# Three orders around the second layer of a two-layer trunk: the last chunk's 1/rms, the spatial mix's banks and the out-projection's parts

## The chip, the core and the metric

The kernel runs on one core of a Trainium2 chip. The metric is the time of one execution in microseconds of device time; the kernel before has a median of 1097.71 us over three runs (1096.62 to 1098.31).

## The reference

1024 prompt tokens and 64 sample tokens, 1088 columns in all, go through two layers and a final RMSNorm. Layer 0 is sparse attention beside a short convolution; layer 1 is a chunked gMLP with a spatial gating unit. What the change touches is the end of layer 0 and all of layer 1:

```python
x = x + gate[:, None] * out                       # end of layer 0
h = _rmsnorm(x, norm_g[1]) * (1 + scale[:, None]) + shift[:, None]
u, v, g = _split(h @ w_in, (SGU_DIM, SGU_DIM, SGU_DIM))
u = jax.nn.gelu(u)
v = _layernorm(jax.nn.gelu(v), ln_g, ln_b)
wm = jnp.tril(ws[:, :lc, :lc])                    # one 128x128 matrix for each of 8 groups
s = jnp.einsum('gij,bnjgc->bnigc', wm, vc) + bs[:, :lc].T[None, None, :, :, None]
out = (u * s * jax.nn.silu(g)) @ w_out
x = x + gate[:, None] * out                       # then the final RMSNorm
```

## The kernel before, in words

Features lie on the 128 partitions, tokens along the free dimension; a tensor of 1024 features is eight slices of 128. Every fp32 operand of a large product is kept as two parts, a high part in fp32r (ScalarE copies it, line 295) and a low part, the difference (VectorE, line 296); a product is three passes, high by high, high by low and low by high. `ah` and `al` hold the two parts of the current activations, 8 slices by 1088 columns.

The program is written in the order of the algorithm, and a planner decides the order of each engine's queue by a simulated time: an earlier instruction of the program goes first if the planner thinks that it is ready, else a later one. `manual_schedule` takes one engine out of this: its instructions stand in the order written. `issue_after(x)` keeps what is written under it behind instruction x. Each engine then runs its queue strictly in order.

**End of layer 0.** `out_projection(0, ...)` (line 1133 on) works on columns 0 to 448, 448 to 832 and 832 to 1088 (chunks 0, 1, 2). For each chunk and each of 8 output tiles come 24 products, the residual on VectorE (line 1153), a square on ScalarE (lines 1156, 1159) and a running sum of the squares on GpSimd (line 1161). `rstd` then sums over the partitions with products against a column of ones (line 229), scales on VectorE (232), takes the power -0.5 on GpSimd (233) and spreads the result over the partitions with transposes (235). `h1` normalises the chunk (lines 1176 to 1181: VectorE, GpSimd, ScalarE, VectorE for each slice) into `ah`, `al` and, in fp32, into the residual's own tiles.

**Sums.** Products of layer 1 after the first two output tiles are made with Strassen's scheme (Winograd's form) on 2 by 2 blocks: seven products in place of eight, of half the depth. The input side needs four sums of blocks: `sums` (VectorE, lines 1220 to 1223) forms them in place, and `sum_parts` splits them into the tiles T1, T2, T3 and, for the fourth, into `ah` and `al`. They come in four pieces of columns, of which the one that reaches into the last chunk is the largest (1024 elements a partition); the other three need only chunks 0 and 1.

**Entry of layer 1.** The first two output tiles (`two`) are made plainly with `project`, 24 products for each of the column ranges 0 to 364, 364 to 728 and 728 to 1088; only the last range needs chunk 2. Then the memory of the residuals is released (`self.resid.close()`), and tiles of layer 1 lie in it, among them S0, S1 and S2, in which `pair_weights` (line 1263, `p_s`) builds the weight sums of the Strassen products. `pair` makes two output tiles with seven products of two halves each ("st", line 1291). Its products go through the PSUM banks "pj", "lg" and "pt" in turn, two banks each.

**Spatial mix.** `v` is transposed to rows, normalised block by block (`layernorm`: statistics on VectorE, power on GpSimd, one product of a column on VectorE, line 1348, and the scaling on ScalarE, line 1351), and `spatial` multiplies, for each of 8 groups, nine blocks by the group's matrix into two banks tagged "lg" and a small one. VectorE evicts them with scale and bias (line 1372); for groups 0 to 3 it goes to an S tile, the same of the three for all parts of a group, and VectorE multiplies it into the gate (line 1374).

**Out-projection of layer 1.** The last pairs make the u tiles, and VectorE multiplies each quarter into the gate product `gs` (line 1466). Then all eight slices of chunk 0, of chunk 1 and of chunk 2 are split into `ah` and `al`, in this order of the program, and `out_projection(1, ...)` runs. Its weights' low parts are made on GpSimd (line 256). The first product of a pair reads slices 0 to 3 of column quarters 0 and 2 of `ah` and `al`, the second slices 4 to 7 of the same quarters, the sixth and the seventh the same slices of quarters 1 and 3; a quarter is 272 columns. The residuals of chunks 1 and 2 are loaded again over SP's queue into tiles that free up at the end.

Of the kernel before, what the change touches and what calls it, by code (L numbers as in the profile page):

```python
# [17 lines left out]
P = 128  # L18
D = 1024
KT = D // P  # L20
# [19 lines left out]
def pieces(w):  # L40

    return [*range(0, w - P, P), w - P]
# [52 lines left out]

OUT_KTS = (4, 5, 6, 7, 0, 1, 2, 3)


# [9 lines left out]
class Trunk:  # L108
# [112 lines left out]

    def rstd(self, name, w, *accs):

        nc = self.nc
        pt = self.bank("pt", name)
        n = len(pieces(w))
        for j, o in enumerate(pieces(w)):
            for i, acc in enumerate(accs):
                nc.tensor.matmul(pt[:, w + j:w + j + 1], acc[:, o:o + P], self.ones, start=i == 0,
                                 stop=i == len(accs) - 1)  # L230
        r = self.small.tile([P, 4], F32, tag="rs", name="rs", bufs=3)
        nc.vector.tensor_scalar(r[:, 0:n], pt[:, w:w + n], 1.0 / D, EPS, op0=OP.mult, op1=OP.add)
        nc.gpsimd.tensor_tensor(r[:, 0:n], r[:, 0:n], self.nhalf[:, 0:n], op=OP.pow)
        for j, o in enumerate(pieces(w)):
            nc.tensor.transpose(pt[:, o:o + P], r[:, j:j + 1].to_broadcast([P, P]), self.ident)
        return pt[:, 0:w]

# [898 lines left out]
    def out_projection(self, l, ws, after):  # L1136
# [4 lines left out]
        for c in range(NCH):  # L1141
# [4 lines left out]
            for t in range(KT):  # L1146
# [10 lines left out]
                else:  # L1157
                    sq = self.column("sq")[:, 0:w]
                    nc.scalar.activation(sq, x[:, t, :], AF.Square)
                    if t < KT - 1 or c < NCH - 1:  # L1160
# [4 lines left out]
            if l == 0:  # L1165
                self.load(self.spill[c], x)
        after(NCH - 1, self.rstd("rstd", *accs[-1]))

# [184 lines left out]
    def spatial(self, g, gs, times):  # L1353

        nc = self.nc
        vt, c = self.vtok[g // 4], slice(g % 4 * P, (g % 4 + 1) * P)
        pt = [self.ps.tile([P, 512], F32, tag="lg", name="sgu_ps", bufs=2) for _ in range(2)]
        for n in range(NBLK):
# [4 lines left out]
        parts = [(slice(a * 512, a * 512 + 512), pt[a].rearrange("p (b c) -> p b c", c=P),  # L1363
                  self.bs[:, g, None, :].to_broadcast([P, 4, P])) for a in range(2)]
        for s, p, b in (*parts, (slice(SO, SO + DEC), ps[:, 0:DEC], self.bs[:, g, 0:DEC])):
            y = gs[:, s]
            if times:
                u = self.l1.tile([P, 512], F32, tag=f"S{g % 3}", name="sgu")[:, 0:s.stop - s.start]
            else:
                u = y  # L1370
            o = u.rearrange("p (b c) -> p b c", c=P) if s.stop <= SEQ else u
            nc.vector.scalar_tensor_tensor(o, p, self.lngb[:, 0, g:g + 1], b, op0=OP.mult, op1=OP.add)
            if times:
                nc.vector.tensor_mul(y, y, u)

    def layer1(self, es):
# [17 lines left out]
        two = [self.weights(w1[t]) for t in range(2)]  # L1394
        for cs in (range(NCH - 1), (NCH - 1,)):
            for t in range(2):
                self.project(two[t], gelu(t), cs)
        self.sum_parts((2, 1, 3))
        self.sum_parts((4,))
        self.resid.close()  # L1400
# [63 lines left out]
        for n, t in enumerate((*range(KT + 4, 2 * KT, 2), *range(2 * KT, 3 * KT, 2))):  # L1464
            def times(src, k, s):
# [4 lines left out]
                                                             name="w_1") if t < 6 else None) for t in range(KT)]  # L1470
        for c in range(NCH):
            s = slice(*OUT_CHUNKS[c])
            for t in range(KT):
                self.split(self.ah[:, t, s], self.al[:, t, s], gs[t][:, s])
        for c in range(1, NCH):
            xc.append(r2.tile([P, KT, w[c]], F32, tag=f"v{c % 2}", name=f"x{c}"))
            self.load(xc[c], self.spill[c])
# [12 lines left out]
    def run(self):  # L1490
        with ExitStack() as es:
# [9 lines left out]
            with self.pool("held", "right") as self.held:  # L1501
# [18 lines left out]
                with self.pool("wo", "right") as wp:  # L1520
# [10 lines left out]
                    with self.tc.issue_after(self.lastav):  # L1531
                        self.out_projection(0, ws, self.h1)
                    self.sums()
            self.layer1(es)
# [72 lines left out]
```

## Time and profile before

| | |
|---|---|
| Median of three runs | 1097.71 us |
| Profiled execution | 1095.83 us, span 1094.1 us |
| Busy: TensorE / VectorE / ScalarE / GpSimd | 1050.8 / 738.5 / 592.5 / 493.5 us |
| Granted TensorE clock | 0.993 of full speed |
| Entry of layer 1 | about 691 to 728 us |
| Spatial mix | about 836 to 860 us |
| End of the last pair, start of the out-projection | about 979 to 1000 us |

In the rows below PE is TensorE, DVE VectorE, ACT ScalarE, POOL GpSimd and SP the engine that issues the transfers. An L number is the line of the kernel that issued the instruction; lines 264 and 295/296 belong to helpers that several stages use, so there the tile's name tells which stage it is. `idle before` is time in which the engine did nothing just before the instruction, and the name behind the arrow is what ended it.

### The profile page before, as it was taken

What the parts mean: (1) busy time and instruction counts of PE and PEld (TensorE: products, weight loads), DVE (VectorE), ACT (ScalarE), POOL (GpSimd) and SP (SyncE); (2) the same over time, 40 slices, a digit from 0 to 9 for tenths busy, and PEclk for the clock granted to TensorE, in tenths of its full rate; (3) what the DMA queues carried; (4) which work ended last, traced back from release to release, by engine and by line L of the source; (5) the groups of instructions that cost most, each with busy time, mean ns of one, the idle gap of its engine ahead of it and who ended that gap; (6) DMA issues with size and microseconds to landing.
All of it is one profiled execution on the core that took longest, in us unless ns stands there. A gap on an engine that the chain in (4) does not pass through costs nothing.

```text
span 1094.1 us, 20011 instructions
## 1 busy us (share of the span) xinstructions
PE 1050.8 (96%) x7523; PEld 1013.6 (93%) x7523; DVE 738.5 (67%) x1849; ACT 592.5 (54%) x1152; POOL 493.5 (45%) x519
## 2 busy tenths in 40 slices
PE   4899999999999989999999999989999999999996
PEld 4889778999999989999999999989999999998996
DVE  5610789998887786777787445685568876667134
ACT  5643488775776597767787323543346244354111
POOL 1014224345864655535458246464334344454322
PEclk9899999999999999999999999999999999999998
DMA  9754711121110111000001622031111311124012
GB/s 366 300 202 155 261 31 36 66 77 39 40 39 21 39 58 30 12 21 20 20 20 40 243 85 97 39 97 59 40 39 31 121 44 43 66 87 154 1 68 96
DMA packets 31776, 90.30 MB, mean 83 GB/s; under 512 B 5568, under 2 KB 11968, under 8 KB 28480
## 3 DMA queue, kind: packets, MB, share of 16 engines
q1 hardware_dynamic: 31680, 89.03, 23.0%
q8 instruction: 59, 0.97, 0.4%
q14 instruction: 37, 0.30, 0.1%
HBM read 78.44 MB, written 10.58 MB: 81 GB/s over the span
## 4 chain that ended last, share of the span: by engine, by line
PE 83%; DVE 9%; ACT 3%; issue 2%; DMA 1%; POOL 1%; SPq 0%; POOLq 0%; DVEq 0%; ACTq 0%
PE st L1291 20%; PE pj L264 20%; PE op L264 15%; PE pj L281 9%; PE av L731 3%; PE logit_ps L687 3%; PE p_ps L713 3%; PE ada_ps L168 2%; PE first L336 2%; PE score_ps L451 1%; DVE al L296 1%; DVE cum L647 1%; PE score_ps L452 1%; DMA x<-in_x 1%; DVE bias L648 1%
## 5 line engine op out<-in xcount | busy, mean ns | idle before, releaser
L256 POOL TENSOR_TENSOR w_lo<-w_raw,w_hi 128x1024 fp32r<-128x1024 f32 x35 | 84.2, 2407 | 160.0 <-ACT w_hi L255 158.0
L264 PE MATMUL pj<-ah,w_hi 128*128 128x364 f32 (+1 forms) x456 | 150.3, 331 | 1.0 <-ACT w_hi L255 1.0
L264 PE MATMUL pj<-al,w_hi 128*128 128x364 f32 (+1 forms) x456 | 150.3, 330 | 0.7 <-DVE al L1181 0.7
L264 PE MATMUL pj<-ah,w_lo 128*128 128x364 f32 (+1 forms) x456 | 149.2, 329 | 0.0
L1291 PE MATMUL st<-ah,p_w 128*128 128x272 f32 x704 | 137.3, 290 | 0.6 <-ACT ring L1390 0.6
L553 DVE TENSOR_SCALAR_CACHE_REDUCE junk<-S,cand 128x512 bf16<-128x512 f32 (+5 forms) x142 | 119.0, 838 | 1.9
L1291 PEld LDWEIGHTS st<-ah,p_w 128*128 128x128 f32 x704 | 111.7, 188 | 1.7 <-ACT ring L1390 0.9
L1258 POOL TENSOR_TENSOR p_w<-p_s,p_w 128x512 fp32r<-128x512 f32 x44 | 58.9, 1341 | 85.7 <-ACT p_w L1257 85.6
L281 PE MATMUL pj<-ah,w_lo 128*128 128x364 f32 (+1 forms) x288 | 95.7, 332 | 0.0
L281 PE MATMUL pj<-ah,w_hi 128*128 128x364 f32 (+1 forms) x288 | 95.5, 332 | 0.0
L281 PE MATMUL pj<-al,w_hi 128*128 128x364 f32 (+1 forms) x288 | 95.3, 331 | 0.0
L580 ACT ACTIVATE junk<-S,cand 128x896 bf16<-128x896 f32 (+2 forms) x78 | 77.7, 996 | 29.5 <-DVE m L583 25.8
L1291 PE MATMUL st<-al,p_w 128*128 128x272 f32 x352 | 92.8, 291 | 0.0
L1153 DVE SCALAR_TENSOR_TENSOR x<-op,mod,x 128x192 f32<-128x192 f32 (+2 forms) x64 | 30.2, 496 | 91.5 <-PE op L264 87.4
L264 PEld LDWEIGHTS pj<-ah,w_hi 128*128 128x128 f32 x456 | 85.6, 188 | 2.0 <-ACT w_hi L255 1.3
L264 PEld LDWEIGHTS pj<-al,w_hi 128*128 128x128 f32 x456 | 85.7, 188 | 1.3 <-DVE al L1181 1.3
L264 PEld LDWEIGHTS pj<-ah,w_lo 128*128 128x128 f32 x456 | 85.6, 188 | 0.2 <-issue 0.2
L264 PE MATMUL op<-ah,w 128*128 128x448 f32 (+2 forms) x336 | 82.4, 330 | 0.8 <-ACT ah L295 0.8
L694 POOL TENSOR_SCALAR S<-S,sm 128x128 f32<-128x128 f32 (+8 forms) x68 | 51.3, 759 | 67.8 <-DVE sm L693 55.9
L1258 POOL TENSOR_TENSOR p_w<-p_raw,p_w 128x512 fp32r<-128x512 f32 x33 | 47.0, 1425 | 47.5 <-ACT p_w L1257 47.5
L1291 PEld LDWEIGHTS st<-al,p_w 128*128 128x128 f32 x352 | 66.3, 188 | 0.3 <-issue 0.2
L264 PE MATMUL op<-ah,w_hi 128*128 128x384 f32 (+2 forms) x200 | 65.1, 326 | 0.0
(320 smaller groups left out, 2998.2 us busy)
## 6 DMA issues: line engine op xcount, KB each, us to landing
ada<-in_ada_w SPq DMA_DIRECT2D x19, 1024.0 KB, 7.8
w_raw<-in_w SPq DMA_DIRECT2D x31, 512.0 KB, 3.5
p_raw<-in_w SPq DMA_DIRECT2D x44, 256.0 KB, 3.0
w_raw<-in_wo SPq DMA_DIRECT2D x16, 512.0 KB, 3.5
x<-in_x SPq DMA_DIRECT2D x8, 544.0 KB, 6.3
bo<-in_ada_w SPq DMA_DIRECT2D x4, 1024.0 KB, 6.7
x<-in_x SPq DMA_DIRECT2D x1, 1792.0 KB, 7.8
spill<-x SPq DMA_DIRECT2D x1, 1792.0 KB, 5.7
```

What stands on the lines that cost most here:

```text
L256: (nc.gpsimd if lo_eng == "pool" else nc.vector).tensor_sub(lo, raw, hi)
L264: last = self.nc.tensor.matmul(ps, wt[:, kt, :], at[:, kt, c0:c1], start=n == 0, stop=n == len(mms) - 1)
L281: self.nc.tensor.matmul(ps, wt[:, kt, :], at[:, kt, a:b], start=kt == 0 and i == 0, stop=kt == KT - 1 and i == 2)
L553: V.tensor_scalar(junks[0][:, 0:SW[j]], self.S[:, span(j)], thr, 0.0, op0=OP.is_lt, op1=OP.add, accum_out=col(cv, j))
L580: nc.scalar.activation(junks[1][:, 0:SW[j]], self.S[:, span(j)], AF.Sign, scale=-1.0, bias=col(cand, j), accum_out=col(cv, j))
L687: nc.tensor.matmul(pt[:, 0:w], lhs, keys[i][:, t // 2, s], start=i == 0, stop=i == 1)
L694: self.lastnorm = nc.gpsimd.tensor_scalar(p, p, st[:, 3:4], 0.5, op0=OP.mult, op1=OP.mult).ins
L713: nc.tensor.transpose(pt[0:r, o:o + P], p[:, j * P:j * P + r], self.ident)
L731: self.lastav = nc.tensor.matmul(av[:, 0:m], self.vs[0:r, vbase + j, t // 2, :], part[0:r, x:x + m], start=j == 0 and i == 0, stop=(j + 1) ...
L1153: nc.vector.scalar_tensor_tensor(x[:, t, a:b], ps[:, a:b], self.mod[l][:, 16 + t, j:j + 1], x[:, t, a:b], op0=OP.mult, op1=OP.add)
L1258: nc.gpsimd.tensor_sub(w[:, 1], src, w[:, 0])
L1291: nc.tensor.matmul(ps, w[:, p, k, :], at[:, k, :], start=i == 0, stop=i == len(mms) - 1)
```

## The change

It has three parts.

First, the end of `rstd` is split: `rstd_steps` stops between the power and the transposes. For layer 0, `out_projection` no longer normalises the last chunk but hands the unfinished `rstd_steps` to layer 1. There the 24 products of the first output tile and the first column range are written out for TensorE one by one; after the seventh come the sums for 1/rms, after the nineteenth the transposes. `h1` of the last chunk and `sums` follow. The other five groups of 24 products come in the order (tile 0, range 1), (1, 0), (1, 1), (0, 2), (1, 2), and all parts of the sums are held behind the last square (`lastsq`), T2 first, then T3, T1 and the fourth.

Second, in `spatial` the odd groups use the two "pj" banks, the multiply into the gate (groups 0 to 3) runs on GpSimd, and the S tiles go round for each part and not for each group.

Third, the parts of chunk 0 for the out-projection are made in two cuts, columns 0 to 272 and 272 to 448, for slices 0 to 5, and whole for slices 7 and 6; the parts of chunks 1 and 2 are held behind the last high part of chunk 0 (`lasthi`).

```diff
+RSTD = (6, 18)
-    def rstd(self, name, w, *accs):
+    def rstd(self, *args):
+        *_, rb = self.rstd_steps(*args)
+        return rb
+
+    def rstd_steps(self, name, w, *accs):
...
         nc.gpsimd.tensor_tensor(r[:, 0:n], r[:, 0:n], self.nhalf[:, 0:n], op=OP.pow)
+        yield
         for j, o in enumerate(pieces(w)):
             nc.tensor.transpose(pt[:, o:o + P], r[:, j:j + 1].to_broadcast([P, P]), self.ident)
-        return pt[:, 0:w]
+        yield pt[:, 0:w]
...
-                    nc.scalar.activation(sq, x[:, t, :], AF.Square)
+                    self.lastsq = nc.scalar.activation(sq, x[:, t, :], AF.Square).ins
...
+        if l == 0:
+            return self.rstd_steps("rstd", *accs[-1])
         after(NCH - 1, self.rstd("rstd", *accs[-1]))
...
-        pt = [self.ps.tile([P, 512], F32, tag="lg", name="sgu_ps", bufs=2) for _ in range(2)]
+        pt = [self.ps.tile([P, 512], F32, tag="pj" if g % 2 else "lg", name="sgu_ps", bufs=2) for _ in range(2)]
...
+        n = g
         for s, p, b in (*parts, (slice(SO, SO + DEC), ps[:, 0:DEC], self.bs[:, g, 0:DEC])):
             y = gs[:, s]
             if times:
-                u = self.l1.tile([P, 512], F32, tag=f"S{g % 3}", name="sgu")[:, 0:s.stop - s.start]
+                n += 1
+                u = self.l1.tile([P, 512], F32, tag=f"S{n % 3}", name="sgu")[:, 0:s.stop - s.start]
...
             if times:
-                nc.vector.tensor_mul(y, y, u)
+                nc.gpsimd.tensor_mul(y, y, u)
...
         two = [self.weights(w1[t]) for t in range(2)]
-        for cs in (range(NCH - 1), (NCH - 1,)):
-            for t in range(2):
-                self.project(two[t], gelu(t), cs)
-        self.sum_parts((2, 1, 3))
-        self.sum_parts((4,))
+
+        with self.tc.manual_schedule(engines={mybir.EngineType.PE}):
+            for n, _ in enumerate(self.steps(two[0], gelu(0), (0,), n=1)):
+                if n in RSTD:
+                    rb = next(self.late)
+        self.h1(NCH - 1, rb)
+        self.sums()
+        for t, cs in ((0, (1,)), (1, (0, 1)), (0, (2,)), (1, (2,))):
+            self.project(two[t], gelu(t), cs)
+        with self.tc.issue_after(self.lastsq):
+            self.sum_parts((2, 3, 1))
+            self.sum_parts((4,))
...
-        for c in range(NCH):
-            s = slice(*OUT_CHUNKS[c])
-            for t in range(KT):
+
+        a, b = OUT_CHUNKS[0]
+        for s, ts in ((slice(a, Q), range(KT - 2)), (slice(Q, b), range(KT - 2)), (slice(a, b), (KT - 1, KT - 2))):
+            for t in ts:
                 self.split(self.ah[:, t, s], self.al[:, t, s], gs[t][:, s])
+        with self.tc.issue_after(self.lasthi):
+            for c in range(1, NCH):
+                s = slice(*OUT_CHUNKS[c])
+                for t in range(KT):
+                    self.split(self.ah[:, t, s], self.al[:, t, s], gs[t][:, s])
...
                     with self.tc.issue_after(self.lastav):
-                        self.out_projection(0, ws, self.h1)
-                    self.sums()
+                        self.late = self.out_projection(0, ws, self.h1)
```

## Rows read from the trace of the kernel before

**Rows 1.** By stage: length, busy PE, PEld, DVE, ACT, POOL; clock, DMA, GB/s.
```profile
705.00:718.00 13.00, 12.27 (x74) 11.49 (x72) 10.77 (x20) 9.42 (x22) 11.15 (x16) 1.00 0.00 0
718.00:728.00 10.00, 6.81 (x53) 6.44 (x52) 9.93 (x10) 6.84 (x13) 4.98 (x4) 1.00 0.04 11
...
836.00:842.30 6.30, 6.30 (x53) 6.11 (x52) 3.33 (x12) 5.30 (x9) 1.08 (x2) 1.00 0.01 3
842.30:860.00 17.70, 16.16 (x122) 14.44 (x121) 17.67 (x37) 1.89 (x3) 3.84 (x3) 1.00 0.04 12
...
983.00:999.70 16.70, 14.06 (x69) 12.18 (x68) 16.70 (x26) 9.53 (x21) 9.09 (x3) 1.00 0.17 58
999.70:1010.00 10.30, 10.30 (x51) 9.50 (x52) 4.16 (x8) 3.17 (x6) 1.85 (x1) 1.00 0.92 356
```

**Rows 2.** Waits of TensorE: total, times, longest, in 690 to 760 and 836 to 1010.
```profile
PE st L1291 <- ACT p_w L1257: 2.6, 1, 2.6
...
PE op L264 <- DVE al L296: 1.8, 1, 1.8
```

**Rows 3.** Timeline of 691 to 705 (start, duration), TensorE, VectorE, ScalarE, GpSimd.
```profile
691.21 0.33 PE L264 MATMUL pj<-ah,w_hi 128*128 128x364 f32 x1
692.38 0.33 PE L264 MATMUL pj<-al,w_hi 128*128 128x364 f32 x1
...
691.83 0.60 DVE L1153 SCALAR_TENSOR_TENSOR x<-op,mod,x 128x192 f32<-128x192 f32 x2
...
695.16 0.40 ACT L1159 ACTIVATE sq<-x 128x256 f32<-128x256 f32 x1
...
699.67 0.16 DVE L232 TENSOR_SCALAR rs<-rstd 128x2 f32<-128x2 f32 x1 [2.42 <-PE rstd L229]
699.91 0.71 POOL L233 TENSOR_TENSOR rs<-rs,nhalf 128x2 f32<-128x2 f32 x1 [8.69 <-DVE rs L232]
704.16 0.75 DVE L1176 TENSOR_TENSOR t<-x,rstd 128x256 f32<-128x256 f32 x2 [4.33 <-PE rstd L235]
```

**Rows 4.** GpSimd's normalisation by line (busy, mean ns); VectorE's timeline behind it.
```profile
L1179 POOL TENSOR_SCALAR x<-t,modA,mod 128x192 f32<-128x192 f32 (+1 forms) x16 | 11.5, 732 | 4.4 <-DVE t L1176 4.4
...
719.37 2.20 DVE L1223 TENSOR_TENSOR x<-x,x 128x1024 f32<-128x1024 f32 x1
726.36 1.28 DVE L1263 TENSOR_TENSOR p_s<-p_raw 128x512 f32<-128x512 f32 x2
```

**Rows 5.** Timeline around the spatial mix, 820 to 861.
```profile
823.48 1.12 DVE L1348 SCALAR_TENSOR_TENSOR mv<-mv 128x1 f32<-128x1 f32 x1
...
837.46 0.74 DVE L1372 SCALAR_TENSOR_TENSOR sgu<-sgu_ps,lngb,misc 128x512 f32<-128x512 f32 x1
...
838.37 3.10 ACT L1351 ACTIVATE vtok<-vtok,mv 128x512 f32<-128x512 f32 x4
...
857.43 3.01 POOL L1258 TENSOR_TENSOR p_w<-p_s,p_w 128x512 fp32r<-128x512 f32 x2 [2.17 <-ACT p_w L1257]
857.98 0.74 DVE L1372 SCALAR_TENSOR_TENSOR gsb<-sgu_ps,lngb,misc 128x512 f32<-128x512 f32 x1
859.55 1.44 DVE L1263 TENSOR_TENSOR p_s<-p_raw,p_s 128x512 f32<-128x512 f32 x1
```

**Rows 6.** Out-projection: VectorE's timeline, a group by shape, SP's issues, a weight's high part.
```profile
990.26 2.60 DVE L1466 TENSOR_TENSOR gsb<-gsb,u 128x272 f32<-128x272 f32 x1
992.78 5.83 DVE L296 TENSOR_TENSOR al<-gsb,ah 128x448 fp32r<-128x448 f32 x8
...
L296 DVE TENSOR_TENSOR al<-gsb,ah 128x256 fp32r<-128x256 f32 x4 | 3.8, 962 | 0.0
...
1001.15 0.33 SPq L130 DMA_DIRECT2D x<-spill  x1
1001.57 0.39 SPq L130 DMA_DIRECT2D w_raw<-in_wo  x1
...
1010.70 1.06 ACT L255 ACTIVATE w_hi<-w_raw 128x1024 fp32r<-128x1024 f32 x1 [1.75 <-DMA w_raw<-in_wo]
```

## The prediction

> **What bounds the kernel now.** I read the page's busy shares first: TensorE (PE) works nearly all the span, so what this change can win is TensorE's idle time in the stages it touches, and no other engine's busy sum. Next I read busy time by stage [rows 1]: a row whose PE figure equals its length has nothing to give. Idle are 13.00 - 12.27 = 0.73 us in 705 to 718 and 10.00 - 6.81 = 3.19 us in 718 to 728 (entry of layer 1: 3.92 together), 17.70 - 16.16 = 1.54 us in 842.3 to 860 (spatial mix), 16.70 - 14.06 = 2.64 us in 983 to 999.7 (start of the out-projection). The sum is 8.1 us. Last I read who ended the long ones [rows 2]: one wait of 2.6 us for the weights of a Strassen product and one of 1.8 us for a low part of the out-projection. In both VectorE's queue stood ahead, as the timelines show [rows 4, 6].
>
> **Entry of layer 1.** Today the last residual is added at 691.83 (until 692.43), but its square runs on ScalarE at 695.16, behind nine parts of the sums (three small pieces, three parts each); the column sums are out at 699.67, and VectorE starts the last chunk's normalisation at 704.16, though the power on GpSimd takes only 0.71 us from 699.91 [rows 3]. Of the 12.3 us from residual to normalisation little is work. The change keeps the parts off ScalarE until the square has been issued and writes TensorE's order out: seven products, sums, twelve products, transposes, five products. The trace has the first product at 691.21 and the eighth at 692.38 [rows 3], 0.167 us apart; the sums stand in the eighth's place. The square can run at 692.43 and takes 0.40, so the sums can start at about 692.9: TensorE, which can take nothing else now, waits 0.5 us. Bounds: 0 if the residual comes sooner, 3.2 us if the square stays at 695.16 + 0.40. I take 0.5, since the residual's row is the nearest. The sums take some 0.6 us, VectorE's scaling and the power end by 694.7 (from 699.67 to 700.62 they took 0.95 now), and the twelve products cover until 695.5. Normalisation then starts near 695.9 instead of 704.16: 8.2 us sooner.
>
> What is late next: GpSimd's part of the normalisation is 16 instructions at 732 ns, 11.5 us [rows 4]. From 695.9, with the nine small parts now beside it, the last chunk is ready between 708 and 712. TensorE has four groups of 24 products, 4 x 24 x 0.167 = 16 us, before it needs the first slice at about 709 and the eighth at 712.5, so I take 0 for that wait (bounds 0 and 2 us). The 0.73 us go. Then VectorE's train: three large differences and four large parts, seven instructions, one of them 2.20 us at 719.37, ended before p_s at 726.36 [rows 4], because p_s lies where the residual chunks lay. That end was 704.16 + 22.2. From 695.9, plus some 3 us for small parts that used to be done before, it comes at about 721, and ScalarE's copy follows. TensorE reaches the third Strassen product at 691.2 + 144 x 0.167 + 0.5 + 1.0 (sums, transposes) = 716.7 and 48 products of 6.81 / 53 = 0.128 [rows 1] on, about 723. I leave 0.8 us of wait for contention in the train. Stage: 3.92 - 0.5 - 0.8 = 2.6 us gained. Bounds: 3.9, and about 0 (the train ending at 726 as now, 3.4 us of wait beside the 0.5); below nothing I see no way, since the train starts sooner in every case.
>
> **Spatial mix.** Until 842.3 TensorE has no gap [rows 1], because the next pair's first 24 products sit in the two "pj" banks and fill the time until ScalarE has the last normalised block (838.37 + 3.10 = 841.47) [rows 5]. Then seven groups alternate over two "lg" banks, and each waits for VectorE: 1.54 us. Afterwards odd groups take the "pj" banks. So evictions no longer stop TensorE: per group it needs 16.16 / 7 = 2.3 us [rows 1], while VectorE, without the multiply, needs two evictions of 0.74 and a small one, under 1.9. But the filler is gone: the next pair's first product has to wait behind the last odd group. In its place from 838 stand the rest of group 0 and seven eighths of group 1 (about 2.3 us) and, once two evictions are through, the first halves of groups 2 and 3 (2 x 1.0 us): 4.3 us, enough for 841.5. Upper bound of the gain 1.5; lower bound -2.7: without those halves TensorE is dry at 840.3 and stands until 841.5, or until 843.0 if one GpSimd instruction stands before the last scale, and the evictions win nothing. The multiply on GpSimd is not in the trace; the nearest row is its subtraction of the same size, 3.01 / 2 = 1.5 us beside VectorE [rows 5]. Eight and four small ones are 12 to 14 us from 838 to about 852, and three "S" tiles and four banks let VectorE run ahead of them; p_s for the next pair then starts near 852, as today. I take +0.6 us, nearer the upper end, because VectorE's first eviction came at 837.46 [rows 5], well before 841, even today.
>
> Is GpSimd free for this? A p_s of two SBUF tiles took 1.44 us at 859.55 while GpSimd's 3.01 ran, the eviction of a PSUM tile 0.74 at 857.98 beside the same instructions, and a product of one column 1.12 us at 823.48 [rows 5]. The Trainium skill (SBUF — State Buffer, Who interferes with whom) says that a VectorE instruction with two SBUF inputs and a GpSimd instruction that reads SBUF exclude each other for a whole instruction, while one SBUF input does not contend; the trace agrees on both counts, with these numbers. By that rule evictions stay at 0.74 and the layer norm's last one-column product can stand behind a multiply, which is rival D; the sum above would then have -1.2 in place of +0.6.
>
> **Out-projection.** At 983 the last pair's products end. Five banks hold what chunk 0 can do with six of eight slices; then TensorE waits for the low part (1.8) and, for the other 0.8, for the high part of the last slices [rows 1, 2]. VectorE's queue shows why: a gate product at 990.26 took 2.60 us beside GpSimd, and then eight parts, several of them chunk 1's and 2's, took 5.83 us from 992.78, ahead of the last gate products, after which ScalarE could start [rows 6]. The change cuts chunk 0 at column 272: columns 0 to 272 of slices 0 to 5 lie in quarters that only the last pair's first two products read, so these six parts can leave the jam: five products of 24 x 0.128 = 3.1 us lie between them and 983, which puts them at about 968; the rest are narrower. Chunks 1 and 2 (16 parts) may not start before the last high part of chunk 0. The gate products of slices 6 and 7 then go through at about 983 to 985, and TensorE needs their parts only six slices, 18 x 0.202 = 3.6 us (10.30 / 51 each [rows 1]), after 983. All 2.64 us can go; 0 would stay if GpSimd's low weights, which are unchanged, hold VectorE as before. I take 2.4, near the upper end, because what stood ahead is moved behind. Six more instructions on ScalarE and on VectorE lie under products.
>
> Other edits: the S tiles' new rotation and the generator cost nothing by themselves, and the two projections in another order are the same 144 products.
>
> **Sum.** 2.6 + 0.6 + 2.4 = 5.6 us. The profiled execution took 1095.83 us (span 1094.1 and 1.7 around it), 1.9 below the median of three, 1097.71; as a difference the sum stands against either: 1090.2 for an execution like the profiled one, 1092.1 for the median.
>
> **Rivals.**
> A, the forecast: all three stages give most of their idle time, 1092.1, own range 1089 to 1095.
> B, the train stays the bound at the entry: sums and parts slowed by GpSimd end 2 us later, and the wait for the third product's weights keeps 2.6 us. For it: 2.20 us at 719.37 for a difference of 1024 columns beside GpSimd [rows 4]; against: they start 8 us sooner. Gain 3.92 - 0.5 - 2.6 = 0.8, in all 0.8 + 0.6 + 2.4 = 3.8: 1093.9.
> C, the out-projection keeps its 2.64 us: the jam is contention with GpSimd's low weights, for which the 2.60 us at 990.26 speaks; against it, that the parts of chunks 1 and 2 leave the jam. Gain 2.6 + 0.6 = 3.2: 1094.5.
> D, the spatial mix loses: without the filler TensorE is dry from 840.3, and a multiply of 1.5 us ahead of the layer norm's last column puts the last block from 841.5 to 843.0. 2.7 lost, 1.5 won: 2.6 + 2.4 - 1.2 = 3.8: 1093.9. For it speaks that the first eviction ends at 838.2 [rows 5], and its multiply is then ready before that column; against, that two evicted banks give TensorE 2 us more.
> E, slower: the parts of chunks 1 and 2, held back, hold a DMA queue. The load of chunk 2's residual goes into the tile that they read; it was issued at 1001.15, the eighth weight's load right behind it at 1001.57, and that weight's high part ran at 1010.70, 9.1 us later [rows 6]. If chunk 0's last high part comes at 999 as now, 16 parts at 0.96 us [rows 6] end at 1014.4, the high part at 1014.8 + 9.1 + 1.1 = 1025.0, and TensorE, with its 2.6 us of waits, is at the eighth weight at 983 + 2.6 + 7 x 24 x 0.202 = 1019.5: 5.5 lost against 2.6 + 0.6 won elsewhere: 1100.0. It decides from an end of the parts at about 1012; from a high part at 985, as I expect it, they end before 1001 and the queue is no later than today.
> F, the change doesn't do what it says: the planner has the parts ahead of the square all the same, TensorE stands 3.2 us at the sums, and the rest stays: 1097.0.
>
> **Numbers.** A 0.54, B 0.12, C 0.12, D 0.08, E 0.10, F 0.04. 0.2% is 2.2 us, about what can be told from no change. A is faster throughout; B to D, with 1.7 us of spread, three times in four, else same: 0.54 + 0.24 = 0.78 faster; 0.08 + F = 0.12 same; E 0.10 slower. The range goes from 1089.0 (8.1 us gone and the median's own 0.6) to 1096.5, above which lie E, F and the edge of B to D, under 2 in 10.
>
> **What would show it.** The sums' wait on the square near 0.5 us; VectorE's normalisation starting 4 to 5 us after the last residual instead of 12; no wait for weights at the third Strassen product over 1 us; no gap between spatial groups, but one before the last normalised block if D holds; six parts of chunk 0 before the last pair's end and no TensorE gap after it. The forecast is wrong if TensorE's idle time moves to other places in these stages, above all to the sums, which nothing else may pass now.

## The result and the profile after

The changed kernel has a median of 1088.2 us over six runs (1087.06 to 1091.1). The kernel before now has six as well, with a median of 1096.26 us (1094.67 to 1098.31); the prediction knew the first three of them, with 1097.71. The ratio is 0.993 with a 95% interval of 0.9911 to 0.9948, so the change makes the kernel about 0.7% faster. The forecast was 1092.1, in a range that began at 1089.0: the direction was right, the gain was larger than forecast, and the median lies 0.8 us below the range.

The profiled execution took 1089.86 us (span 1088.1), 6.0 us less than the one of before. A table of stages, worked out from TensorE's rows, says more than the two spans. Each column runs from one fixed product of TensorE to the next. The last one ends where TensorE leaves the chain of work that ended last (1081.10 before, 1075.09 after); in both kernels 24 products of another tile still follow, 2.86 us. I use these lengths in all that follows; each comes from one profiled execution.

| TensorE's stages, us | first product of layer 1 at | from it to the first spatial product | from there to the first product of the out-projection | from there to its last product on that chain |
|---|---|---|---|---|
| before | 691.21 | 144.89 | 146.98 | 98.02 |
| after | 692.79 | 141.08 | 145.91 | 95.31 |
| gained | -1.58 | 3.81 | 1.07 | 2.71 |

The three stages gave 7.6 us together. The execution that was profiled had reached layer 1 1.58 us later. As far as the two traces show it, TensorE's queue is the same in both kernels up to there, and the delay is nearly as old as the execution: the transposes into `ada_ps` stood at 23.57 and 34.66 before and at 25.69 and 36.54 now. The other profiled kernels below reach layer 1 between 689.7 and 693.1.

Busy time by stage, in the kernel after, in windows of the same lengths as those of before [rows 1] and put where the same work now runs. The columns are the same: length, TensorE, its weight loads, VectorE, ScalarE, GpSimd, granted clock, DMA share, GB/s.

```profile
706.60:719.60 13.00, 12.73 (x80) 12.37 (x79) 11.67 (x16) 9.16 (x18) 7.75 (x9) 1.00 0.00 0
719.60:729.60 10.00, 10.00 (x82) 9.85 (x81) 9.70 (x12) 4.65 (x10) 6.98 (x6) 1.00 0.47 135
833.80:840.10 6.30, 6.30 (x49) 5.74 (x49) 2.75 (x12) 5.26 (x9) 2.88 (x5) 1.00 0.01 3
840.10:857.80 17.70, 17.06 (x134) 15.90 (x133) 14.50 (x25) 1.86 (x3) 13.45 (x12) 1.00 0.09 31
979.70:996.40 16.70, 16.66 (x82) 14.87 (x82) 16.41 (x28) 11.73 (x26) 7.62 (x4) 1.00 0.50 185
996.40:1006.70 10.30, 10.30 (x52) 9.44 (x51) 4.87 (x5) 2.38 (x4) 3.85 (x3) 1.00 0.43 153
```

TensorE's idle time was 0.73 + 3.19 + 1.54 + 2.64 = 8.1 us; it is 0.27 + 0.64 + 0.04 = 0.95 us. The waits of TensorE from layer 1 to the end, in the kernel after (total, times, longest):

```profile
PE rstd L235 <- ACT x L1166: 1.1, 1, 1.1
PE rstd L242 <- POOL rs L239: 1.0, 1, 1.0
PE sgu_ps L1368 <- DVE sgu L1383: 0.6, 1, 0.6
PE st L1300 <- ACT ring L1401: 0.3, 1, 0.3
PE vs_ps L1343 <- DVE vtok L1341: 0.2, 1, 0.2
```

The first two belong to the final norm at the very end and were there before. The wait of 2.6 us for the third Strassen product's weights and that of 1.8 us for a low part of the out-projection [rows 2] have no row any more.

**Entry of layer 1.** From the timeline of 692 to 702 in the kernel after, against [rows 3]:

```profile
692.79 0.33 PE L288 MATMUL pj<-ah,w_hi 128*128 128x364 f32 x1
693.96 0.33 PE L271 MATMUL pj<-ah,w_hi 128*128 128x364 f32 x1
...
695.46 0.28 PE L235 MATMUL rstd<-ones,acc 128*128 128x1 f32 x2
...
697.17 0.28 PE L235 MATMUL rstd<-ones,sq 128*128 128x1 f32 x2
...
700.82 0.38 PE L242 MATMUL rstd<-ident,rs 128*128 128x128 f32 x2
...
693.41 0.60 DVE L1160 SCALAR_TENSOR_TENSOR x<-op,mod,x 128x192 f32<-128x192 f32 x2
...
694.10 0.42 ACT L1166 ACTIVATE sq<-x 128x256 f32<-128x256 f32 x1 [2.46 <-DVE x L1160]
...
699.05 0.15 DVE L238 TENSOR_SCALAR rs<-rstd 128x2 f32<-128x2 f32 x1
...
701.24 0.75 DVE L1185 TENSOR_TENSOR t<-x,rstd 128x256 f32<-128x256 f32 x2 [1.63 <-PE rstd L242]
```

The square now follows the last residual at once. The written products have line 288, all others line 271: after seven written ones come nine of another group, then the first sums; 24 others stand ahead of the transposes in all. So the written order holds among the written instructions, and others may still stand between them. The normalisation starts 8.45 us after the first product; it was 12.95 [rows 3].

What comes behind it, from the timelines of VectorE, ScalarE and TensorE around the third Strassen product, against [rows 4]:

```profile
718.80 2.32 DVE L303 TENSOR_TENSOR T2l<-x,T2h 128x1024 fp32r<-128x1024 f32 x1
721.04 2.45 DVE L303 TENSOR_TENSOR al<-x,ah 128x64 fp32r<-128x64 f32 x2
723.41 1.28 DVE L1272 TENSOR_TENSOR p_s<-p_raw 128x512 f32<-128x512 f32 x2
...
724.73 1.15 ACT L1266 ACTIVATE p_w<-p_s 128x512 fp32r<-128x512 f32 x2 [1.46 <-DVE p_s L1272]
...
725.47 0.37 PE L1300 MATMUL st<-T3h,p_w 128*128 128x272 f32 x1
```

The train is out 30.6 us after the first product of layer 1 (35.15 before), and the third product starts with no wait. From the start of the normalisation to `p_s` the train takes 22.2 us, as before: it starts 4.5 us sooner and ends 4.5 us sooner.

**Spatial mix.** GpSimd, VectorE and TensorE around the last normalised block, against [rows 5]:

```profile
836.05 1.55 POOL L1385 TENSOR_TENSOR ring<-ring,sgu 128x512 f32<-128x512 f32 x2 [0.93 <-DVE sgu L1383]
837.56 0.54 POOL L1356 TENSOR_TENSOR mv<-mv,nhalf 128x1 f32<-128x1 f32 x1
838.06 0.33 POOL L1385 TENSOR_TENSOR ring<-ring,sgu 128x64 f32<-128x64 f32 x1
841.03 7.98 POOL L1385 TENSOR_TENSOR ring<-ring,sgu 128x512 f32<-128x512 f32 x8 [2.64 <-DVE sgu L1383]
...
838.13 0.27 DVE L1357 SCALAR_TENSOR_TENSOR mv<-mv 128x1 f32<-128x1 f32 x1 [0.50 <-POOL mv L1356]
840.20 1.41 DVE L1383 SCALAR_TENSOR_TENSOR sgu<-sgu_ps,lngb,misc 128x512 f32<-128x512 f32 x2 [1.79 <-PE sgu_ps L1368]
...
841.00 7.70 PE L1368 MATMUL sgu_ps<-misc,vtok 128*128 128x128 f32 x64 [0.62 <-DVE sgu L1383]
```

TensorE has one gap of 0.62 us; then 64 products run without a stop, where the groups waited for VectorE five times before. VectorE has idle time again.

**Out-projection.** Parts, gate products and loads around 983, against [rows 6]:

```profile
961.21 0.78 DVE L303 TENSOR_TENSOR al<-gsb,ah 128x272 fp32r<-128x272 f32 x2
...
976.07 2.29 DVE L1484 TENSOR_TENSOR gsb<-gsb,u 128x272 f32<-128x272 f32 x1
978.28 1.09 DVE L303 TENSOR_TENSOR al<-ring,ah 128x176 fp32r<-128x176 f32 x4
...
985.63 0.78 DVE L1484 TENSOR_TENSOR gsb<-gsb,u 128x272 f32<-128x272 f32 x2
...
986.09 0.58 ACT L302 ACTIVATE ah<-gsb 128x448 fp32r<-128x448 f32 x1 [2.49 <-DVE gsb L1484]
...
998.74 0.33 SPq L132 DMA_DIRECT2D x<-spill  x1
```

The six wide cuts of chunk 0 are made at 961 to 964, the narrow ones from 978, the last gate products run at 985.63, and the last high part of chunk 0 at 986.09. TensorE's first product of the out-projection is at 979.78, and no later one waits.

### The profile page after: what moved, and what is told of

Same layout as the page of the kernel before. It is cut to its first block, busy times and chain, and to the rows that moved or that the text cites. A ratio compares the mean times of both kernels' runs of the same rounds, so it can differ in the third digit from the quotient of the medians.

```text
span 1088.1 us, 20024 instructions
## 1 busy us (share of the span) xinstructions
PE 1052.1 (97%) x7523; PEld 1015.4 (93%) x7523; DVE 735.1 (68%) x1843; ACT 593.2 (55%) x1158; POOL 503.9 (46%) x531
## 4 chain that ended last, share of the span: by engine, by line
PE 87%; DVE 5%; ACT 3%; issue 2%; DMA 1%; POOL 1%; SPq 0%; POOLq 0%; DVEq 0%; ACTq 0%
PE st L1300 21%; PE pj L271 19%; PE op L271 17%; PE pj L288 10%; PE av L738 3%; PE logit_ps L694 3%; PE p_ps L720 3%; PE ada_ps L170 2%; PE first L343 2%; PE score_ps L458 2%; PE sgu_ps L1368 1%; PE score_ps L459 1%; DVE cum L654 1%; DMA x<-in_x 1%; DVE bias L655 1%
```

## The experiments

The theory: each stage gives back its own idle time, the entry because the train starts earlier, the spatial mix because evictions no longer stop TensorE, the out-projection because the parts of chunks 1 and 2 leave VectorE's queue. The rivals: one part does it all; the order written out, or the cuts, do nothing; the new waits that I had reserved are there and hidden. All numbers are ratios to the kernel before on the same chip, with 95% intervals, and the stage lengths of the table above. Between kernels that have the same code in a stage, the entry repeats to 0.34 us (141.00 to 141.34) and the spatial mix to 0.02. The out-projection does not: it takes 97.86 to 98.53 us with the order of before, and with the whole third part 95.15 to 95.34 in seven kernels, but 96.24 and 96.41 in two.

**The change once more, and each part alone.** The whole change again, in a second series, beside three kernels that keep one part each.

> The changed kernel again, beside the three parts alone on the same chip. Theory (each stage gives back the TensorE idle time that it loses, and no more): 7.6 us faster than before, the sum of 3.8 (entry), 1.1 (spatial mix) and 2.7 (out-projection) by which the stages between the same marks are shorter in the two profiles. Rival (the 6.0 us between the two profiled executions are the whole gain, and the 8.1 us between the medians hold about 2 us of drift from one set of runs to another): 6.0 us.

> The kernel before with the first part alone (split 1/rms, written order, parts held behind the last square). Theory: 3.8 us faster, with no TensorE wait for weights at the third Strassen product; from the first product of layer 1 to the spatial mix's first product 141 us in place of 144.9, and the stages behind it as long as before. Rival (the later stages absorb it, since VectorE sets them): under 2 us, the idle time of the spatial mix or of the out-projection grows by the rest. The prediction's own term: 2.6 us.

The first part alone: the other two are undone.

```diff
-        pt = [self.ps.tile([P, 512], F32, tag="pj" if g % 2 else "lg", name="sgu_ps", bufs=2) for _ in range(2)]
+        pt = [self.ps.tile([P, 512], F32, tag="lg", name="sgu_ps", bufs=2) for _ in range(2)]
...
-                n += 1
...
-                nc.gpsimd.tensor_mul(y, y, u)
+                nc.vector.tensor_mul(y, y, u)
...
-        for s, ts in ((slice(a, Q), range(KT - 2)), (slice(Q, b), range(KT - 2)), (slice(a, b), (KT - 1, KT - 2))):
+        for s, ts in ((slice(a, b), range(KT)),):
...
-        with self.tc.issue_after(self.lasthi):
+        with nullcontext():
```

> The kernel before with the second part alone (four banks, multiply on GpSimd, S tiles by part). Theory: 1.1 us faster, one TensorE wait of about 0.6 us left before group halves 2 and 3, none between the groups behind it. Rival D of the prediction (the filler is lost): 0 to 1.2 us slower. The prediction's own term: 0.6 us.

The second part alone: the third is undone as above, and the first so:

```diff
-        if l == 0:
-            return self.rstd_steps("rstd", *accs[-1])
...
-        with self.tc.manual_schedule(engines={mybir.EngineType.PE}):
...
-            self.project(two[t], gelu(t), cs)
-        with self.tc.issue_after(self.lastsq):
-            self.sum_parts((2, 3, 1))
-            self.sum_parts((4,))
+        for cs in (range(NCH - 1), (NCH - 1,)):
+            for t in range(2):
+                self.project(two[t], gelu(t), cs)
+        self.sum_parts((2, 1, 3))
+        self.sum_parts((4,))
...
-                        self.late = self.out_projection(0, ws, self.h1)
+                        self.out_projection(0, ws, self.h1)
+                    self.sums()
```

> The kernel before with the third part alone (chunk 0's parts in two cuts, chunks 1 and 2 held). Theory: 2.7 us faster, no TensorE wait over 0.1 us between the last pair and the end of chunk 0's products. Rival C (GpSimd's low weights hold VectorE as before): under 1 us. The prediction's own term: 2.4 us.

The third part alone: the first and the second are undone, by the same lines.

| | ratio | entry and pairs | spatial mix and pairs | out-projection |
|---|---|---|---|---|
| before | 1 | 144.89 | 146.98 | 98.02 |
| all again | 0.9937 [0.9924, 0.9949] | 141.03 | 145.90 | 95.15 |
| first part alone | 0.9959 [0.9946, 0.9971] | 141.00 | 146.98 | 98.53 |
| second alone | 0.9989 [0.998, 0.9998] | 144.86 | 145.91 | 97.86 |
| third alone | 0.9982 [0.9973, 0.9991] | 144.93 | 146.97 | 96.41 |

The medians of the second series differ by 6.7 us, 5.6 to 8.3 by the interval, which does not decide between the theory's 7.6 and its rival's 6.0; the stages of its profile gave 7.8. Each part gives its gain in its own stage, 3.9, 1.1 and 1.6 us alone, and the other stages stay as they were, but for the out-projection of the first part alone, 0.5 us longer for a reason that I have not found. The first two parts have the same worth in company. The third is worth 2.7 to 2.9 with both others, and the 2.7 us that I had expected of it alone fell: it gave 1.6. The traces show why; VectorE and then GpSimd, in the third part alone:

```profile
981.97 3.28 DVE L303 TENSOR_TENSOR al<-ring,ah 128x176 fp32r<-128x176 f32 x4
...
982.32 2.49 POOL L263 TENSOR_TENSOR w<-w_raw,w 128x1024 fp32r<-128x1024 f32 x1 [0.57 <-ACT w L262]
```

The four narrow parts took 3.28 us beside a low weight on GpSimd; in the kernel after they took 1.09, in a gap between two low weights, and the gate product ahead of them bore the collision (2.29 us at 976.07), where nothing waited. TensorE waits 0.6 us for a low part here and not at all there. That the part stands alone is not the reason. e6 below has all three parts, but for one multiply in the spatial mix, and meets the same collision:

```profile
977.42 3.28 DVE L303 TENSOR_TENSOR al<-ring,ah 128x176 fp32r<-128x176 f32 x4
```

Its out-projection takes 96.24 us. In the seven kernels that have the whole third part and take 95.15 to 95.34, the four narrow parts took 1.08 or 1.09. So a collision like that goes with about 1 us; which instruction meets it changes with edits in other stages.

**Entry: does the train have slack?** The prediction let the normalisation come 8.2 us sooner and reserved 0.8 us of wait at the end of the train; it came 4.5 us sooner and no wait was left for the weights. One of the two must then be wrong about slack: either the train has some, or its end lies just at the third product. Three kernels move the start of the normalisation by different means.

> The changed kernel without the hold of the sum parts behind the last square. In TensorE's queue the column sums then end behind 31 of the first products and the transposes stand behind 56; in the changed kernel behind 25 and 43. Theory (VectorE's train from the last normalisation to p_s has no slack left, so each us by which 1/rms comes later is a us of wait at the third Strassen product): transposes 13 products x 0.167 = 2.2 us later, from the first product of layer 1 to the spatial mix 1.5 to 2.2 us longer than the changed kernel's 141.0 us. Rival (the hold is not needed, the written order does it): within 0.3 us of 141.0.

```diff
-        with self.tc.issue_after(self.lastsq):
+        with nullcontext():
```

> The changed kernel with TensorE's order at the entry left to the planner (same program, no written order). The sums stand where they do in the changed kernel (behind 16 and 25 products), the transposes behind 57 in place of 43. Theory (no slack): 14 x 0.167 = 2.3 us later, the entry 1.5 to 2.3 us longer than 141.0 us. Rival (the planner's late transposes are absorbed, the gain came from the hold and the program's order): within 0.3 us.

```diff
-        with self.tc.manual_schedule(engines={mybir.EngineType.PE}):
+        with nullcontext():
```

> The changed kernel with two groups of 24 products written out for TensorE in place of one, the column sums behind the seventh product with nothing between, and the transposes behind the second group (48 products). This tests the prediction's own step: the sums stand at 1.2 us from the first product, the square ends about 1.7 us from it, so TensorE waits about 0.5 us at the sums. Theory (no slack): transposes 48 x 0.167 + 0.6 + 0.5 = 9.1 us from the first product in place of 8.0, so the entry is 0.5 + 1.1 less what the wait itself covers: 0.8 to 1.6 us longer than 141.0. Rival (slack of a us or more in VectorE's train): only the 0.5 us.

```diff
-                if n in RSTD:
-                    rb = next(self.late)
+                if n == RSTD[0]:
+                    next(self.late)
+            for n, _ in enumerate(self.steps(two[0], gelu(0), (1,), n=1)):
+                pass
+            rb = next(self.late)
...
-        for t, cs in ((0, (1,)), (1, (0, 1)), (0, (2,)), (1, (2,))):
+        for t, cs in ((1, (0, 1)), (0, (2,)), (1, (2,))):
```

| | ratio | first "p_s" after the first product of layer 1 | entry and pairs |
|---|---|---|---|
| after | 0.993 [0.9911, 0.9948] | 30.6 | 141.08 |
| e10, transposes behind 24 more written products | 0.9938 [0.9917, 0.996] | 31.9 | 142.40 |
| e4, parts not behind the square | 0.9949 [0.9932, 0.9966] | 32.6 | 143.08 |
| e5, no written order | 0.9934 [0.9912, 0.9956] | 32.75 | 143.24 |

The ratios can't tell these apart, the stages can: 1.3 us later is 1.3 us longer, 2.0 is 2.0, 2.1 is 2.2, each within what was expected. For delays of this size the train has no slack. The longest of the waits are not at the weights, because other work stands in the same queues behind the train. ScalarE and TensorE in e4:

```profile
691.16 0.80 ACT L302 ACTIVATE T2h<-x 128x704 fp32r<-128x704 f32 x1 [1.35 <-PE op L271]
...
694.90 0.40 ACT L1166 ACTIVATE sq<-x 128x256 f32<-128x256 f32 x1
...
717.68 0.39 PE L1300 MATMUL st<-ah,p_w 128*128 128x272 f32 x1 [1.07 <-ACT ring L1401]
...
725.58 0.27 PE L1343 MATMUL vs_ps<-ident,ring 128*64 128x128 f32 x1 [1.23 <-DVE vtok L1341]
```

Without the hold the nine parts go ahead of the square again, as before. TensorE then stands 1.07 us at the first Strassen product, for a bank that ScalarE empties late, and 1.23 us at a transpose, for a copy that VectorE makes behind the first "p_s". In e10 the written order is tight, with nothing between the seven products and the sums, and TensorE waits 0.3 us there for the square:

```profile
PE rstd L235 <- ACT sq L1166: 0.3, 1, 0.3
```

That is the wait for which the prediction had reserved 0.5.

**Spatial mix: the banks or the engine?**

> The changed kernel with the multiply into the gate back on VectorE (four banks and the S tiles' rotation stay). Theory (four banks alone do not do it: VectorE needs 2 x 0.74 + 2 x 0.65 + 0.5 = 3.2 us for each of the first four groups and TensorE 2.3): from the spatial mix's first product to the out-projection's first 0.5 to 2 us longer than the changed kernel's 145.9 us. Rival (banks are all, VectorE catches up on the last four groups): within 0.2 us of 145.9, or less, since GpSimd no longer delays the layer norm's last power.

```diff
-                nc.gpsimd.tensor_mul(y, y, u)
+                nc.vector.tensor_mul(y, y, u)
```

> The changed kernel with all groups of the spatial mix in the two 'lg' banks again; the multiply stays on GpSimd. Theory (VectorE's multiply was what kept the two banks occupied; without it an eviction of 0.74 us fits beside the other bank's 1.0 us of products, and the filler comes back): TensorE's waits between the groups 0.3 us or less, the stage 145.5 to 146.2 us against 145.9 in the changed kernel and 147.0 before. Rival (two banks are the limit): 146.5 to 147.0 us.

```diff
-        pt = [self.ps.tile([P, 512], F32, tag="pj" if g % 2 else "lg", name="sgu_ps", bufs=2) for _ in range(2)]
+        pt = [self.ps.tile([P, 512], F32, tag="lg", name="sgu_ps", bufs=2) for _ in range(2)]
```

In what follows "with four banks alone" means that the multiply is back on VectorE (e6), "with GpSimd alone" that the groups are back in two banks (e7). The stage takes 147.47 us with four banks alone (0.9951 [0.9934, 0.9967]) and 151.24 with GpSimd alone (0.9964 [0.9953, 0.9976]), against 146.98 before and 145.91 with both. Each half loses by itself. With the banks alone, TensorE waits 1.9 us in three places for evictions behind which VectorE still multiplies. With GpSimd alone I had expected 145.5 to 146.2, and that fell. Windows of 840 to 850 and a row of TensorE in that kernel:

```profile
840.00:843.00 3.00, 1.53 (x12) 1.14 (x10) 1.34 (x2) 0.00 (x0) 1.26 (x1) 1.00 0.00 0
843.00:846.00 3.00, 2.78 (x13) 2.78 (x14) 1.54 (x3) 0.00 (x0) 2.50 (x2) 0.56 0.00 0
846.00:850.00 4.00, 3.78 (x28) 3.40 (x26) 1.81 (x7) 0.00 (x0) 3.09 (x4) 0.90 0.00 0
```

```profile
843.22 5.66 PE L1368 MATMUL sgu_ps<-misc,vtok 128*128 128x128 f32 x32 [0.84 <-DVE sgu L1383]
```

TensorE and VectorE take turns on two banks, and TensorE waits 3.9 us in seven places where the kernel after waits 0.6. Busy for 1.53 of 3.00 us, TensorE is then granted 0.56 of its clock, that is, 1.2 GHz, the lower of its two levels, for most of the stretch, and 32 products take 5.66 us (177 ns each); in the kernel after 64 take 7.70 (120 ns each). That is 3.3 us of waits and 32 x 0.057 = 1.8 us of clock, 5.1 of the 5.3 us that the stage lost against the kernel after. Against before, where VectorE had the multiplies as well, the 4.3 us are 2.4 us more of waits and the same 1.8 us of clock. Why the waits grew is not settled. What the trace shows is a later start: VectorE's second eviction of 512 columns begins 7.80 us after the stage's first product (840.41), where it began after 5.60 us in the kernel before (841.70).

**What is the last 0.6 us in the spatial mix?** A large and a small multiply stand ahead of the last layer norm's power on GpSimd (836.05, 837.56). The theory was that they delay the last normalised block.

> The changed kernel with GpSimd's multiplies held behind the layer norm's last power; in the changed kernel two of them (1.55 us) stand ahead of it, and ScalarE waits 0.8 us for the last scale. Theory (that delay makes the one TensorE wait of 0.6 us that is left in the spatial mix): the stage 0.3 to 0.6 us shorter than 145.9 us, under 0.6% faster than before in all by 0.5 us more than the changed kernel. Rival (the wait is for the eviction of the banks, whatever the layer norm does): within 0.2 us of 145.9, or longer, since the multiplies start later.

```diff
-        nc.gpsimd.tensor_tensor(mv[r, 2:3], mv[r, 2:3], self.nhalf[r, 0:1], op=OP.pow)
+        self.lastmv = nc.gpsimd.tensor_tensor(mv[r, 2:3], mv[r, 2:3], self.nhalf[r, 0:1], op=OP.pow).ins
...
-                nc.gpsimd.tensor_mul(y, y, u)
+                with self.tc.issue_after(self.lastmv):
+                    nc.gpsimd.tensor_mul(y, y, u)
```

The stage takes 145.57 us, 0.34 less than after; the ratio is 0.9922 [0.9906, 0.9938], the lowest of all, though its interval does not part it from the change as it is. The number is the expected one, but the reason is not. VectorE, GpSimd and TensorE in this kernel:

```profile
835.72 1.22 DVE L1357 SCALAR_TENSOR_TENSOR mv<-mv 128x1 f32<-128x1 f32 x1 [0.75 <-POOL mv L1356]
...
838.37 1.41 DVE L1383 SCALAR_TENSOR_TENSOR sgu<-sgu_ps,lngb,misc 128x512 f32<-128x512 f32 x2 [1.12 <-PE sgu_ps L1368]
...
835.65 2.00 POOL L1386 TENSOR_TENSOR ring<-ring,sgu 128x512 f32<-128x512 f32 x3
...
837.17 1.39 PE L1368 MATMUL sgu_ps<-misc,vtok 128*128 128x128 f32 x8
838.49 0.43 PE L1371 MATMUL sgus_ps<-misc,vtok 64*128 64x64 f32 x2
839.18 7.70 PE L1368 MATMUL sgu_ps<-misc,vtok 128*128 128x128 f32 x64 [0.26 <-DVE sgu L1383]
```

The power ended 0.9 us sooner, but the product of one column behind it took 1.22 us beside the multiply that now follows (0.27 in the kernel after, where only a multiply of 64 columns, 838.06, ran beside it), and it ended 4.57 us after the stage's first product, in the kernel after 4.53. The last block came no sooner. What changed is TensorE's order: two small products moved behind the large ones, and VectorE's second eviction of 512 columns began 6.00 us after the stage's first product (838.37) and not 6.33 (840.20). That is the 0.34 us. I had the right size for the wrong reason, by luck.

**Out-projection: the hold or the cuts?**

> The changed kernel without the hold of chunks 1 and 2 behind chunk 0's last high part; the two cuts of chunk 0 stay. Theory (what cost the 2.7 us was VectorE doing parts of chunks 1 and 2 ahead of the last gate products): the wait comes back, from the out-projection's first product to TensorE's last 1.5 to 2.7 us longer than the changed kernel's 95.2 us. Rival (the cuts alone take chunk 0 out of the jam): within 0.3 us of 95.2.

```diff
-        with self.tc.issue_after(self.lasthi):
+        with nullcontext():
```

> The changed kernel with chunk 0's parts whole (eight of 448 columns, slices 0 to 7 in order) and chunks 1 and 2 still held. Theory (the hold is most of it): 0 to 1 us longer than 95.2 us, by a wait for a low part of slices 4 to 7. Rival (the six early parts are most of it): 1.5 us longer or more.

```diff
-        for s, ts in ((slice(a, Q), range(KT - 2)), (slice(Q, b), range(KT - 2)), (slice(a, b), (KT - 1, KT - 2))):
+        for s, ts in ((slice(a, b), range(KT)),):
```

Without the hold the stage takes 96.89 us (0.994 [0.9923, 0.9956]), without the cuts 95.92 (0.9936 [0.9918, 0.9954]), with both 95.31. The hold is worth 1.6 us, as expected. The 0.6 us without the cuts lie within what was expected too, but they are not shown to be the cuts' worth: there two whole parts took 3.00 us beside a low weight (977.36), and with the cuts in place e3 and e6, which meet such a collision, take 96.41 and 96.24. Without the hold the old picture is back; a wait of TensorE, and then VectorE's parts of chunks 1 and 2 ahead of chunk 0's last gate products:

```profile
PE op L271 <- DVE al L303: 1.5, 1, 1.5
```

```profile
979.80 3.55 DVE L303 TENSOR_TENSOR al<-ring,ah 128x256 fp32r<-128x256 f32 x4
...
989.48 0.78 DVE L1484 TENSOR_TENSOR gsb<-gsb,u 128x272 f32<-128x272 f32 x2
```

## Why the prediction was right in its mechanism and short in its size

The forecast was rival A, and A is what happened: all three stages gave most of their idle time. The sum was 5.6 us; the stages gave 7.6. The terms were mis-sized, the entry most.

- **Entry, 2.6 forecast, 3.81 measured: the term that failed.** It was 3.92 less two reserves, for waits that did not come. The 0.5 us at the sums rested on "TensorE, which can take nothing else now"; TensorE took nine products of another group (693.96 to 695.46), by which time the square was done. e10 shows what the tight order costs: 0.3. The 0.8 us at the third product rested on contention in the train, and nothing waits for those weights. The step between was wrong too, the other way: the normalisation came 4.5 us sooner in place of 8.2, because 24 other products stood ahead of the transposes and VectorE's scaling at 699.05 stood behind six of the low parts. Against that, the 3 us that I had added for the small parts did not come, since these ran ahead of the normalisation. The two errors met, by luck: the train ended 30.6 us after the first product, where I had 29.8, and TensorE came to the third product after 32.7, where I had 31.8. e4, e5 and e10 show that this fits with nothing to spare.
- **Spatial mix, 0.6 forecast, 1.07 measured.** Evictions stop TensorE once (0.62) in place of five times. Rival D had a gap of 2.7 about there, for the last normalised block; e11 left 0.26 of the 0.62 though that block came no sooner. The multiplies took 1.55 + 0.33 + 7.98 + 1.68 = 11.5 us on GpSimd (12 to 14 forecast). Neither half of the edit has this gain (e6, e7), which the prediction did not see.
- **Out-projection, 2.4 forecast, 2.71 measured.** The six cuts came at 961, not 968. The last high part of chunk 0 came at 986.09 (985 forecast), the parts of chunks 1 and 2 ended at 998.7 (before 1001 forecast).
- **The rivals.** B and C did not happen, and neither did F: the square ran at 694.10, ahead of the parts. E had its mechanism right but not its case: the load of chunk 2's residual was issued at 998.74, as the held parts ended, but that is 2.4 us sooner than before [rows 6].
- **The Trainium skill's rule on the ports.** I weighed the Trainium skill (SBUF — State Buffer, Who interferes with whom) for the spatial mix: a VectorE instruction with two inputs in SBUF and a GpSimd instruction that reads SBUF shut each other out, and one with a single such input is not stopped. The traces agree: evictions stay at 0.74 us beside the multiplies, and the one-column product took 1.22 us beside one of 512 columns (e11), 0.27 beside one of 64 columns and 0.15 or 0.16 with none beside it.
- **The time itself.** Of the 9.5 us between 1097.71 and 1088.2, 2.0 are the mis-sized terms beyond the 5.6, and 1.45 are the base: three runs had the median 1097.71, six have 1096.26. The range's low end allowed all 8.1 us of idle time and 0.6 for the median, but not a base that was 1.45 too high. In the second series, five runs of the same change had the median 1089.6.

## What to carry to other kernels

Idle time of the engine that bounds the kernel, read stage by stage, told the size of this gain better than the reserves subtracted from it: price a new wait only after looking for work that the order still lets in. Where two edits lift two limits of one loop (here banks and an engine), neither is worth its half alone, and an engine made to take turns can lose its clock as well. Compare stages between fixed instructions, not spans, when executions differ by more than the effect, and look at how far a stage repeats between kernels that share its code before a half microsecond is put down to an edit.

## What the runs showed of the hardware

- TensorE's granted clock can fall inside a long busy kernel: 0.56 in 843 to 846 of e7, after 3.00 us in which TensorE was busy for 1.53; it was 0.90 in the next 4 us. In e6, where TensorE waited 1.9 us in three places, it stayed at 1.00.
- A product of one column on VectorE took 1.22 us where a GpSimd multiply of 512 columns ran beside it, 0.27 beside one of 64 columns, and 0.15 or 0.16 with none: its length went with the neighbour's.
- Four VectorE subtractions of 176 columns took 3.28 us beside a GpSimd subtraction of 1024 columns (e3, e6) and 1.09 between two of them, and the stage around them took about 1 us more or less with it.
- The fourteen profiled executions differ by up to 3.4 us in the time at which layer 1 begins (689.7 to 693.1). The entry and the spatial mix repeat to 0.34 us where the code is the same, the out-projection to 0.7 us with the order of before and to 1.3 us with the whole third part.
